# Every third low part of the mixers' streamed weights moves from VectorE to GpSimd

## The chip, the cores and the metric

The kernel runs on one core of a Trainium2 chip. The core's engines each run their own queue of instructions in order: TensorE (PE in the profile, its weight loads PEld) multiplies matrices, VectorE (DVE), ScalarE (ACT) and GpSimd (POOL) do elementwise work, SyncE (SP) issues transfers. They wait for each other through semaphores. The metric is the device time of one execution in microseconds (us), before and after the change.

## What is computed

The reference runs four layers of a transformer in fp32 on 256 tokens of width 1024 (and 256 context tokens in the first two layers). Two layers come from a diffusion-like model with modulated norms, each of a half FFN, a mixer and another half FFN; two come from a decoder with squared-ReLU MLPs. Cut to what matters:

```python
x, ctx = half_ffn(x), half_ffn(ctx)
x += gate * mixer_ab(...)              # AB: grouped attention and latent attention
x = half_ffn(half_ffn(x))
x += gate * mixer_cd(...)              # CD: gated linear recurrence and neighbourhood attention
x = half_ffn(x)                        # the end of the first block
x = x + cat(nsa_attention(rope(rmsnorm(h @ a_w_in))), memory_attention(...)) @ a_w_out   # NSA
x = x + square(relu(rmsnorm(x) @ w_up)) @ w_down
x = x + cat(dilated_attention(rope(...)), memory_attention(...)) @ b_w_out               # DIL
x = x + square(relu(rmsnorm(x) @ w_up)) @ w_down
```

All projections in it are products of activations with weights that are read once from HBM.

## The kernel before

**Products.** A matmul in fp32 is made of three in the type float32r, which TensorE takes faster. Each operand is split into a high part and a low part, its rest: `h` is the value cast to float32r, `l` the value minus `h`. `mm3` (L326) then adds `h.h`, `h.l` and `l.h` into one PSUM tile (L328 to L330 in the profile; with `wh`, `wl` the two parts of weights and `xh`, `xl` those of activations).

**Streamed weights.** `weight` (L310) fetches a unit of up to 1024 columns with one DMA into a tile `raw` (L306, on SP's queue) and cuts it into slices of up to 512 columns. For each slice, `split` (L299) has ScalarE copy the high part `wh` (L300) and VectorE subtract the low part `wl` (L301). There are three buffers `raw`, and nine each of `wh` and `wl` (`RAW, WBUFS = 3, 9`). A buffer `raw` may be loaded again when both parts of its slices have been made; a buffer `wl` may be filled again when the matmuls that read it are done. The whole kernel makes 1064 low parts of weights.

**Stages.** The program runs ada and the first FFNs, then mixer AB (375 to 640 us of the span), two FFNs, mixer CD (1365 to 1740), an FFN, mixer NSA (1905 to 2090), an MLP, mixer DIL (2285 to 2470), and a last MLP. FFNs and MLPs are long rows of matmuls. The mixers have short chains between the engines as well: norms of heads (`ssq`, `ssk` by VectorE's `sumsq_heads`, `rsy`, `rsa` for the reciprocal root), `bmul` (L770) for the scaling of heads, `gmul` and `rope` (L775, L790: products with the sine at L797, with the cosine at L778, the sum at L805 or, written twice over, at L808), transposes at L814, softmax and attention.

**NSA around 1965 us.** Its keys are projected from the weights `n_g1`; `rest` (L1789) takes the heads' norm `rk` from VectorE (`norm_of`, L1664) and has GpSimd scale both halves `kx` and rotate them into the free residual tile `xr1` (twelve instructions on GpSimd: two at L773, ten in four ropes). TensorE meanwhile multiplies with the next weights `n_g2` (units of 768 columns, cut to slices of 384), and does two smaller jobs: the compression's products (`at<-raw,PT`, L1851, whose weights `n_w1` also go through a `raw` buffer, but are not split) and the attention to memory (`at<-mk,qa`, L882; `po<-PT,mv`, L906). Then come the weights `n_g3`, in slices of 512.

**DIL around 2315 us.** Query heads and keys come in two halves of tokens each. `heads` (L2147) gives the first half's scaling and rope to GpSimd and the second half's to VectorE (`eng[t]`).

**Who sets the order.** The code calls the instructions in one order; a scheduler then reorders them per engine, by its own estimate of what is ready when, and only a few places are pinned by `keep_in_program_order`. So where a low part stands in its engine's queue isn't written in the code. On the chip every engine runs its list strictly in order.

Of the kernel before, what the change touches and what calls it, by code (L numbers as in the profile page):

```python
# [3 lines left out]

# [1 line left out]

# [4 lines left out]
F32 = mybir.dt.float32  # L11
# [4 lines left out]
ALU = mybir.AluOpType  # L16
# [220 lines left out]
class Later:  # L237
    def __init__(self, make):
        self.make, self.made = make, None
# [7 lines left out]
class Kern:  # L247
    def __init__(self, tc, es, a):
        self.tc, self.nc, self.es, self.a = tc, tc.nc, es, a
        self.const = self.pool("const", 1)  # L250
        self.res = self.pool("res", 1)
        self.wp = self.pool("wp", WBUFS)
        self.st = self.pool("st", 4)
        self.sq = self.pool("sq", 2)
        self.ps = self.pool("ps", 3, space=PSUM)
        self.ident = self.const.tile([P, P], F32, name="ident")
        self.gv = self.const.tile([P, 13, KC], F32, name="gv")
        self.cols = self.const.tile([P, 3], F32, name="cols")
        self.ones = self.cols[:, 0:1].to_broadcast([P, P])
        self.flip = False  # L260
        self.filler = iter(())
        self.norms = []
        self.logs = False
        self.xr = [self.res.tile([P, KC, 256], F32, name=f"xr{h}") for h in range(2)]
        self.xh = self.res.tile([P, KC, 512], F32R, name="xh")
        self.xl = self.res.tile([P, KC, 512], F32R, name="xl")
# [29 lines left out]

    def split(self, h, l, src):  # L299
        self.nc.scalar.copy(h, src)  # L300
        self.nc.vector.tensor_tensor(l, src, h.bitcast(F32), op=ALU.subtract)  # L301

    def raw(self, ap=None, n=1024):
        r = self.wp.tile([P, 1024], F32, name="raw", tag="raw", bufs=RAW)[:, :n]
# [4 lines left out]
    def weight(self, ap, cut=512):  # L309

        n = ap.shape[-1]
        r = self.raw(ap, n)
        parts = []
        for c0 in range(0, n, cut):
            m = min(cut, n - c0)
            h, l = (self.wp.tile([P, 512], F32R, name=x, tag=x)[:, :m] for x in ("wh", "wl"))
            self.split(h, l, r[:, c0 : c0 + m])
            parts.append((h, l))

        def at(c):  # L320
            j = c.start // cut
            return [v[:, c.start - j * cut : c.stop - j * cut] for v in parts[j]]

        return at
# [1949 lines left out]
def program(tc, a):  # L2274
    with ExitStack() as es:
        k = Kern(tc, es, a)
        with ExitStack() as ada:
            k.ada_start(ada)
            k.begin()
            k.ffn(0, 0, 2, (0, 1), (0, 2, 3, 2), (0, 3, 9, 2))  # L2280
            k.mixer_ab()
            k.ffn(0, 1, 2, (1, 0), (1, 0, 5, 2))
            k.ffn(1, 0, 2, (1, 1), (1, 5, 9, 1))
        k.mixer_cd()
        k.mem_open()
        k.filler = k.mem_steps(0)
        k.ffn(1, 1, 1, None)
        k.mixer_nsa()
        k.filler = k.mem_steps(1)
        k.mlp(0)  # L2290
        k.mixer_dil()
        k.mlp(1)
        for d in range(KC):
            tc.nc.sync.dma_start(a["out"][:, d], k.xr[0][:, d])
# [19 lines left out]
```

## Time and profile before

| | |
|---|---|
| median of 3 runs | 2627.84 us (2619.73 to 2628.19) |
| the profiled execution | 2626.76 us |
| its span in the profile | 2625.0 us |
| mean granted clock of TensorE | 0.982 |
| TensorE, VectorE, ScalarE, GpSimd busy | 2508.2, 1797.3, 1258.7, 405.7 us |

The span runs from the first instruction to the last. An engine's busy time counts only its own work, so the rest of the span is waiting. The trace also has each instruction's start, length and, in brackets, the idle time before it with what ended that. Rows that carry several instructions of one kind (x2, x8) give the time from the start of the first to the end of the last.

### The profile page before, as it was taken

The numbers are of one execution on the slowest core, as the hardware profiler recorded it, in microseconds if no ns is written. First come the engines' busy times: TensorE is split into PE (matmuls) and PEld (weight loads), VectorE is DVE, ScalarE is ACT, GpSimd is POOL, SyncE is SP. The second block draws the span as 40 slices with busy tenths as digits, with TensorE's granted clock in tenths as the row PEclk, the third lists the DMA queues.
The fourth block names the chain that finished last, engine by engine and source line by source line (L and its number), as shares of the span: only waits on it lengthen the run. The fifth ranks groups of instructions, "written<-read, shape, count | busy, mean of one in ns | idle before, by whom it ended". The sixth has DMA issues, their size and how long they took to land. (4 is left out here: it accounts for less than half of the span.)

```text
span 2625.0 us, 40838 instructions
## 1 busy us (share of the span) xinstructions
PE 2508.2 (96%) x14931; PEld 2163.8 (82%) x14931; DVE 1797.3 (68%) x3664; ACT 1258.7 (48%) x2646; POOL 405.7 (15%) x457
## 2 busy tenths in 40 slices
PE   6999999999999999999999998989998899988999
PEld 4888888777888888788888887789986789977999
DVE  4999536787997336843336568866677776788765
ACT  3332235665423234233236667555555665665653
POOL 3000004201100003000003234120023211132111
PEclk7999999999999999999999999999998999999999
DMA  7777332120675334843333221346652255542554
GB/s 267 229 236 233 121 95 67 55 66 28 219 241 169 96 97 134 284 126 98 97 97 93 89 85 33 98 142 197 185 181 86 70 189 185 180 146 71 180 185 145
DMA packets 114474, 367.23 MB, mean 140 GB/s; under 512 B 13600, under 2 KB 23776, under 8 KB 112864
## 3 DMA queue, kind: packets, MB, share of 16 engines
q1 hardware_dynamic: 114272, 364.61, 43.5%
q8 instruction: 118, 1.93, 0.3%
q14 instruction: 84, 0.69, 0.1%
HBM read 363.51 MB, written 1.05 MB: 139 GB/s over the span
## 5 line engine op out<-in xcount | busy, mean ns | idle before, releaser
L300 ACT CAST wh<-raw 128x512 fp32r<-128x512 f32 (+3 forms) x1064 | 636.8, 608 | 905.4 <-PE ps L329 737.4
L301 DVE TENSOR_TENSOR wl<-raw,wh 128x512 fp32r<-128x512 f32 (+3 forms) x1064 | 741.9, 705 | 425.0 <-ACT wh L300 408.4
L329 PE MATMUL ps<-xl,wh 128*128 128x256 f32 (+1 forms) x2384 | 794.2, 334 | 11.9 <-POOL xl L573 5.1
L328 PE MATMUL ps<-xh,wh 128*128 128x256 f32 (+1 forms) x2384 | 791.1, 334 | 14.4 <-ACT xh L566 4.2
L330 PE MATMUL ps<-xh,wl 128*128 128x256 f32 (+1 forms) x2384 | 790.3, 332 | 0.9 <-DVE wl L301 0.9
L329 PEld LDWEIGHTS ps<-xl,wh 128*128 128x128 f32 x2384 | 456.5, 192 | 60.8 <-POOL xl L573 7.4
L328 PEld LDWEIGHTS ps<-xh,wh 128*128 128x128 f32 x2384 | 454.7, 192 | 61.0 <-ACT wh L300 5.1
L330 PEld LDWEIGHTS ps<-xh,wl 128*128 128x128 f32 x2384 | 456.4, 192 | 43.5 <-DVE wl L301 2.1
L328 PE MATMUL ps<-hh,wh 128*128 128x256 f32 (+1 forms) x1312 | 416.6, 318 | 3.9 <-ACT hh L300 3.9
L329 PE MATMUL ps<-hl,wh 128*128 128x256 f32 (+1 forms) x1312 | 416.6, 318 | 0.2
L330 PE MATMUL ps<-hh,wl 128*128 128x256 f32 (+1 forms) x1312 | 415.8, 317 | 0.0
L520 POOL TENSOR_TENSOR acc<-acc,sq 128x256 f32<-128x256 f32 x119 | 98.2, 827 | 1387.3 <-ACT sq L519 1382.7
L446 DVE CUSTOM_DVE_ANT_0 prod<-aw,crow,adab 128x1024 f32<-128x1024 f32 x224 | 287.3, 1282 | 8.1 <-DMA aw<-ada_t 6.6
L328 PEld LDWEIGHTS ps<-hh,wh 128*128 128x128 f32 x1312 | 247.9, 189 | 21.5 <-ACT hh L300 4.3
L329 PEld LDWEIGHTS ps<-hl,wh 128*128 128x128 f32 x1312 | 247.9, 189 | 18.5 <-DVE hl L301 1.4
L330 PEld LDWEIGHTS ps<-hh,wl 128*128 128x128 f32 x1312 | 247.9, 189 | 16.9
L328 PE MATMUL ps<-wh,xh 128*128 128x512 f32 (+4 forms) x464 | 179.5, 387 | 1.9 <-ACT xh L1583 1.9
L329 PE MATMUL ps<-wl,xh 128*128 128x512 f32 (+4 forms) x464 | 176.8, 381 | 4.2 <-DVE wl L301 4.2
L330 PE MATMUL ps<-wh,xl 128*128 128x512 f32 (+4 forms) x464 | 175.6, 379 | 0.0
L592 DVE SCALAR_TENSOR_TENSOR xr<-ps,hgate,xr 128x256 f32<-128x256 f32 x168 | 75.5, 480 | 74.9 <-PE ps L330 74.4
L300 ACT CAST hh<-s 128x256 fp32r<-128x256 f32 (+1 forms) x158 | 76.9, 487 | 58.7 <-DVE s L642 49.8
L329 PEld LDWEIGHTS ps<-wl,xh 128*128 128x128 f32 x464 | 88.1, 190 | 20.4 <-DVE wl L301 7.1
(490 smaller groups left out, 2747.6 us busy)
## 6 DMA issues: line engine op xcount, KB each, us to landing
raw<-w SPq DMA_DIRECT2D x240, 512.0 KB, 3.7
aw<-ada_t SPq DMA_DIRECT2D x128, 512.0 KB, 4.2
raw<-m_up SPq DMA_DIRECT2D x64, 512.0 KB, 4.1
raw<-m_down SPq DMA_DIRECT2D x64, 512.0 KB, 3.9
raw<-w SPq DMA_DIRECT2D x32, 384.0 KB, 3.8
row<-ada_w SPq DMA_DIRECT2D x8, 1024.0 KB, 13.2
raw<-d_q SPq DMA_DIRECT2D x12, 512.0 KB, 3.7
raw<-ab_g SPq DMA_DIRECT2D x8, 512.0 KB, 3.6
```

Of the source, the lines that this page charges most:

```text
L300: self.nc.scalar.copy(h, src)
L301: self.nc.vector.tensor_tensor(l, src, h.bitcast(F32), op=ALU.subtract)
L328: mm(out, lh, rh, start=start, stop=False)
L329: mm(out, lh, rl, start=False, stop=False)
L330: mm(out, ll, rh, start=False, stop=stop)
L446: v.tensor_tensor_reduce(prod, w, self.crow[:, s], 1.0, self.adab[:, l, j : j + 1], op0=ALU.mult, op1=ALU.add, accum_out=self.mods[l][:, m ...
L520: self.nc.gpsimd.tensor_tensor(acc, acc, t, op=ALU.add)
L592: self.nc.vector.scalar_tensor_tensor(x, pt, gate[:, d : d + 1], x, op0=ALU.mult, op1=ALU.add)
```

## The change

`split` takes an engine for the low part. `weight` counts its slices while a flag says that a mixer's code is being written, and gives the low part of every third of these to GpSimd (`nc.gpsimd`). A context manager sets the flag around the four mixers' calls. High parts stay on ScalarE, all other low parts on VectorE, and nothing else in the code changes. Line numbers of the new file are higher by 1 from L261 on, by 8 or 9 from `raw` on: L301 becomes L302, `mm3`'s lines L337 to L339, L773 becomes L782, L778 L787, L797 L806, L805 L814, L808 L817, L882 L891, L906 L915, L1851 L1860.

```diff
--- before.py
+++ after.py
@@ -1,6 +1,6 @@
 import itertools
 import math
-from contextlib import ExitStack
+from contextlib import ExitStack, contextmanager
 
 import numpy as np
 
@@ -258,6 +258,7 @@
         self.cols = self.const.tile([P, 3], F32, name="cols")
         self.ones = self.cols[:, 0:1].to_broadcast([P, P])
         self.flip = False
+        self.mixing, self.slices = False, itertools.count()
         self.filler = iter(())
         self.norms = []
         self.logs = False
@@ -296,9 +297,16 @@
 
 
 
-    def split(self, h, l, src):
+    def split(self, h, l, src, eng=None):
         self.nc.scalar.copy(h, src)
-        self.nc.vector.tensor_tensor(l, src, h.bitcast(F32), op=ALU.subtract)
+        (eng or self.nc.vector).tensor_tensor(l, src, h.bitcast(F32), op=ALU.subtract)
+
+    @contextmanager
+    def mixer(self):
+
+        self.mixing = True
+        yield
+        self.mixing = False
 
     def raw(self, ap=None, n=1024):
         r = self.wp.tile([P, 1024], F32, name="raw", tag="raw", bufs=RAW)[:, :n]
@@ -314,7 +322,8 @@
         for c0 in range(0, n, cut):
             m = min(cut, n - c0)
             h, l = (self.wp.tile([P, 512], F32R, name=x, tag=x)[:, :m] for x in ("wh", "wl"))
-            self.split(h, l, r[:, c0 : c0 + m])
+            third = self.mixing and next(self.slices) % 3 == 2
+            self.split(h, l, r[:, c0 : c0 + m], self.nc.gpsimd if third else None)
             parts.append((h, l))
 
         def at(c):
@@ -2278,17 +2287,21 @@
             k.ada_start(ada)
             k.begin()
             k.ffn(0, 0, 2, (0, 1), (0, 2, 3, 2), (0, 3, 9, 2))
-            k.mixer_ab()
+            with k.mixer():
+                k.mixer_ab()
             k.ffn(0, 1, 2, (1, 0), (1, 0, 5, 2))
             k.ffn(1, 0, 2, (1, 1), (1, 5, 9, 1))
-        k.mixer_cd()
+        with k.mixer():
+            k.mixer_cd()
         k.mem_open()
         k.filler = k.mem_steps(0)
         k.ffn(1, 1, 1, None)
-        k.mixer_nsa()
+        with k.mixer():
+            k.mixer_nsa()
         k.filler = k.mem_steps(1)
         k.mlp(0)
-        k.mixer_dil()
+        with k.mixer():
+            k.mixer_dil()
         k.mlp(1)
         for d in range(KC):
             tc.nc.sync.dma_start(a["out"][:, d], k.xr[0][:, d])
```

In the order of instructions, 82 low parts leave VectorE's list (1064 before, 982 left) for GpSimd's: 67 of 512 columns, 13 of 384 to 420 and 2 of 256; by mixer 17 in AB, 27 in CD, 18 in NSA, 20 in DIL. The scheduler sets other instructions in a new order as well, mostly by a few places. Three places follow. A name's number tells its tile apart from others of that name.

GpSimd in NSA, before, from the end of the first rope of the keys: the chain `kx`, then the copies `hv` of the compression.

```order
L808 TENSOR_TENSOR xr1_77<-kx_18731,P_18834 128x384
L808 TENSOR_TENSOR xr1_77<-kx_18731,P_18838 128x384
L797 TENSOR_TENSOR P_18843<-kx_18819,ts_18351 128x192
L797 TENSOR_TENSOR P_18847<-kx_18819,tw_18354 128x192
L778 TENSOR_TENSOR kx_18819<-kx_18819,ts_18351 128x192
L778 TENSOR_TENSOR kx_18819<-kx_18819,tw_18354 128x192
L808 TENSOR_TENSOR xr1_77<-kx_18819,P_18843 128x384
L808 TENSOR_TENSOR xr1_77<-kx_18819,P_18847 128x384
L1869 COPY hv_19055<-hT_19053 128x12x16 x2
```

GpSimd there after:

```order
L817 TENSOR_TENSOR xr1_77<-kx_18731,P_18834 128x384
L817 TENSOR_TENSOR xr1_77<-kx_18731,P_18838 128x384
L806 TENSOR_TENSOR P_18843<-kx_18819,ts_18351 128x192
L806 TENSOR_TENSOR P_18847<-kx_18819,tw_18354 128x192
L787 TENSOR_TENSOR kx_18819<-kx_18819,ts_18351 128x192
L787 TENSOR_TENSOR kx_18819<-kx_18819,tw_18354 128x192
L817 TENSOR_TENSOR xr1_77<-kx_18819,P_18843 128x384
L817 TENSOR_TENSOR xr1_77<-kx_18819,P_18847 128x384
L302 TENSOR_TENSOR wl_18884<-raw_18877,wh_18883 128x384
L302 TENSOR_TENSOR wl_19062<-raw_19059,wh_19061 128x512
L302 TENSOR_TENSOR wl_19076<-raw_19069,wh_19075 128x512
L302 TENSOR_TENSOR wl_19092<-raw_19089,wh_19091 128x512
```

The low part `wl_18884` (weights `n_g2`) and three of `n_g3` now stand between the chain and `hv`; two more low parts stand ahead of the chain.

TensorE in NSA, before: the first product with `wl_18884` stands ahead of a group of L1851.

```order
L329 MATMUL ps_18973<-wl_18870,xh_78 128x384
L330 MATMUL ps_18973<-wh_18869,xl_79 128x384
L328 MATMUL ps_18973<-wh_18873,xh_78 128x384
L329 MATMUL ps_18897<-wl_18884,xh_78 128x384
L1851 MATMUL at_18618<-raw_18910,PT_18531 64x256
L1851 MATMUL at_18618<-raw_18910,PT_18533 64x256
L1851 MATMUL at_18618<-raw_18910,PT_18531 64x256
L1851 MATMUL at_18618<-raw_18910,PT_18533 64x256
L330 MATMUL ps_18897<-wh_18883,xl_79 128x384
L328 MATMUL ps_18897<-wh_18889,xh_78 128x384
L329 MATMUL ps_18897<-wl_18890,xh_78 128x384
L330 MATMUL ps_18897<-wh_18889,xl_79 128x384
```

TensorE there after:

```order
L915 MATMUL po_18921<-PT_18803,mv_15582 64x256
L915 MATMUL po_18921<-PT_18764,mv_15583 64x256
L915 MATMUL po_18921<-PT_18803,mv_15583 64x256
L891 MATMUL at_18956<-mk_15904,qa_18946 128x256 x4
L338 MATMUL ps_18973<-wl_18874,xh_78 128x384
L339 MATMUL ps_18973<-wh_18873,xl_79 128x384
L891 MATMUL at_18998<-mk_15963,qa_18947 128x256 x3
L1860 MATMUL at_18618<-raw_18910,PT_18531 64x256
L1860 MATMUL at_18618<-raw_18910,PT_18533 64x256
L1860 MATMUL at_18618<-raw_18910,PT_18531 64x256
L1860 MATMUL at_18618<-raw_18910,PT_18533 64x256
L338 MATMUL ps_18897<-wl_18884,xh_78 128x384
```

The first product with `wl_18884` has moved back, behind three products of `po`, seven of `at<-mk,qa`, a pair with the weights 18873 and 18874 and the group with `raw_18910`.

GpSimd in DIL, before: the rope of the first half's keys `x_23075`, then that of the queries `x_23213`.

```order
L337 TENSOR_TENSOR rsy_23082<-ssv_23079,cols_75 128x2
L773 TENSOR_TENSOR x_23075<-x_23075,rsy_23092 128x512
L797 TENSOR_TENSOR P_23101<-x_23075,tk_22992 128x512
L778 TENSOR_TENSOR x_23075<-x_23075,tk_22992 128x512
L808 TENSOR_TENSOR xr1_77<-x_23075,P_23101 128x1024
L773 TENSOR_TENSOR x_23213<-x_23213,rsy_23217 128x512
```

GpSimd there after:

```order
L346 TENSOR_TENSOR rsy_23082<-ssv_23079,cols_75 128x2
L302 TENSOR_TENSOR wl_23155<-raw_23148,wh_23154 128x512
L302 TENSOR_TENSOR wl_23171<-raw_23168,wh_23170 128x512
L782 TENSOR_TENSOR x_23075<-x_23075,rsy_23092 128x512
L806 TENSOR_TENSOR P_23101<-x_23075,tk_22992 128x512
L787 TENSOR_TENSOR x_23075<-x_23075,tk_22992 128x512
L817 TENSOR_TENSOR xr1_77<-x_23075,P_23101 128x1024
L302 TENSOR_TENSOR wl_23185<-raw_23178,wh_23184 128x512
L302 TENSOR_TENSOR wl_23314<-raw_23311,wh_23313 128x512
L302 TENSOR_TENSOR wl_23328<-raw_23321,wh_23327 128x512
L782 TENSOR_TENSOR x_23213<-x_23213,rsy_23217 128x512
L806 TENSOR_TENSOR P_23226<-x_23213,tq0_22995 128x512
```

Two low parts stand ahead of the keys' rope and three behind it; `wl_23185` follows its last instruction.

On SP the loads keep their places nearly everywhere. That of `raw_18940` (`n_w1`), the third load after `raw_18877` (the source of `wl_18884`), waits for GpSimd besides VectorE now, and the loads of `raw_18986` and of the weights `n_g3` stand behind it.

## Rows read from the trace of the kernel before

**Rows 1.** The page, part 1: each engine's busy time, share, instructions.

```profile
PE 2508.2 (96%) x14931; PEld 2163.8 (82%) x14931; DVE 1797.3 (68%) x3664; ACT 1258.7 (48%) x2646; POOL 405.7 (15%) x457
```

**Rows 2.** Windows, NSA, DIL, sum: length, PE, PEld, DVE, ACT, POOL busy, clock, DMA.

```profile
1905.00:2090.00 185.00, 164.80 (x991) 130.01 (x989) 137.79 (x433) 102.75 (x270) 45.82 (x55) 0.92 0.35 112
2285.00:2470.00 185.00, 167.46 (x1062) 144.17 (x1062) 155.82 (x367) 116.88 (x263) 53.53 (x62) 0.97 0.41 131
sum 1010.00, PE 935.42 PEld 773.18 DVE 748.31 ACT 618.75 POOL 278.62; mean PE 233.85 PEld 193.30 DVE 187.08 ACT 154.69 POOL 69.66
```

**Rows 3.** Waits of TensorE in NSA: total, times, longest.

```profile
PE ps L328 <- DVE ssq L745: 3.8, 1, 3.8
```

**Rows 4.** TensorE's timeline in DIL: start, length, instruction, idle before and releaser.

```profile
2314.23 0.50 PE L329 MATMUL ps<-wl,xh 128*128 128x512 f32 x1 [0.96 <-DVE wl L301]
...
2322.11 0.90 PE L814 MATMUL at<-ident,xr 128*128 128x128 f32 x3 [3.61 <-DVE xr L808]
...
2345.36 0.50 PE L329 MATMUL ps<-wl,xh 128*128 128x512 f32 x1 [0.87 <-DVE wl L301]
```

**Rows 5.** VectorE's groups by line and shape: busy us, mean ns of one.

```profile
L301 DVE TENSOR_TENSOR wl<-raw,wh 128x512 fp32r<-128x512 f32 x984 | 702.5, 720 | 417.1 <-ACT wh L300 401.0 <-PE ps L330 8.3
```

**Rows 6.** GpSimd's timeline in DIL, ropes of two `x`.

```profile
2315.39 2.73 POOL L808 TENSOR_TENSOR xr<-x,P 128x1024 f32<-128x1024 f32 x1
...
2344.83 1.61 POOL L805 TENSOR_TENSOR x<-x,P 128x512 f32<-128x512 f32 x1
```

**Rows 7.** VectorE's timeline in DIL, two pairs of low parts.

```profile
2312.41 3.46 DVE L301 TENSOR_TENSOR wl<-raw,wh 128x512 fp32r<-128x512 f32 x2
...
2325.28 1.29 DVE L301 TENSOR_TENSOR wl<-raw,wh 128x512 fp32r<-128x512 f32 x2
```

**Rows 8.** GpSimd's groups by line and shape, 512 and 384 columns.

```profile
L773 POOL TENSOR_TENSOR x<-x,rsy 128x512 f32<-128x512 f32 x4 | 5.3, 1324 | 29.5 <-DVE rsy L345 22.1 <-ACT wh L300 7.4
...
L808 POOL TENSOR_TENSOR xr<-kx,P 128x384 f32<-128x384 f32 x4 | 4.5, 1134 | 0.0
```

**Rows 9.** GpSimd's timeline in NSA, start and end of the `kx` chain.

```profile
1964.99 2.54 POOL L773 TENSOR_TENSOR kx<-kx,rk 128x384 f32<-128x384 f32 x2 [21.49 <-DVE rk L1667]
...
1973.92 2.50 POOL L808 TENSOR_TENSOR xr<-kx,P 128x384 f32<-128x384 f32 x2
```

**Rows 10.** VectorE's timeline in NSA, around `rk`.

```profile
1964.22 0.54 DVE L301 TENSOR_TENSOR wl<-raw,wh 128x384 fp32r<-128x384 f32 x1
1964.68 0.17 DVE L1667 COPY rk<-rsy 128x12 f32<-128x12 f32 x1
```

**Rows 11.** TensorE's timeline in NSA, around the first use of `wl_18884`.

```profile
1964.90 0.33 PE L328 MATMUL ps<-wh,xh 128*128 128x384 f32 x1
1965.07 0.34 PE L329 MATMUL ps<-wl,xh 128*128 128x384 f32 x1
1965.34 1.08 PE L1851 MATMUL at<-raw,PT 128*64 128x256 f32 x8
...
1967.43 1.08 PE L906 MATMUL po<-PT,mv 128*64 128x256 f32 x6
...
1968.89 0.62 PE L882 MATMUL at<-mk,qa 128*128 128x256 f32 x4
...
1970.92 0.51 PE L882 MATMUL at<-mk,qa 128*128 128x256 f32 x3
1972.15 1.08 PE L1851 MATMUL at<-raw,PT 128*64 128x256 f32 x8 [0.72 <-DMA raw<-n_w]
...
1976.93 0.39 PE L329 MATMUL ps<-wl,xh 128*128 128x512 f32 x1
```

**Rows 12.** DMA issues: count, KB each, median us from issue to landing.

```profile
raw<-n_w SPq DMA_DIRECT2D x8, 512.0 KB, 4.0
```

**Rows 13.** Windows of 10 us in DIL, same columns.

```profile
2310.00:2320.00 10.00, 7.07 (x30) 5.06 (x28) 9.42 (x13) 6.14 (x12) 6.87 (x4) 1.00 0.50 158
2320.00:2330.00 10.00, 7.89 (x36) 6.68 (x37) 8.50 (x18) 5.20 (x12) 4.35 (x3) 0.83 0.48 152
```

## The prediction

> **What bounds the kernel now.** I read the table of engines first, then the windows of the four mixers, then the waits and the timelines of single engines there. TensorE is busy for 96% of the span, VectorE for 68%, GpSimd for 15% [rows 1]. So a change of low parts can win only what TensorE idles, and lose whatever it makes TensorE wait. The windows narrow this to the mixers: over their 1010 us TensorE is busy for 935.42 us and idles for 1010 - 935.42 = 74.6 us, while VectorE is busy for 748.31 us (74%) and GpSimd for 278.62 us (28%) [rows 2]. In NSA's window 185 - 164.80 = 20.2 us are idle, in DIL's 185 - 167.46 = 17.5 us. The longest single waits are for small VectorE work at the end of a chain, such as 3.8 us for a sum of squares [rows 3], and 3.61 us for `xr` in DIL [rows 4]. TensorE runs its matmuls in a fixed order, so one late low part holds everything behind it.
>
> **What the change removes from VectorE.** The order of the changed kernel has 82 low parts on GpSimd, 67 of them of 512 columns. One takes VectorE 0.72 us [rows 5], so at most 82 x 0.72 = 59 us leave it, 59/748 = 7.9% of its work in the mixers. If all of TensorE's idle time there were VectorE's and shrank in that share, 0.079 x 74.6 = 5.9 us would come back. That is the far end of this term. The near end is none, because GpSimd's work seems to slow VectorE's: in DIL two low parts took 3.46 us while GpSimd worked on `x`, and two took 1.29 us when it was free for most of them [rows 6, 7]. GpSimd gets 82 more instructions. Nothing of their form and width (two operands from SBUF, a subtraction into float32r, 512 columns) stands on GpSimd before; the nearest by width are a 512-column product at 1.32 us and a 384-column sum at 1.13 us [rows 8], so 82 x 1.32 = 108 us at most, on an engine that idles for 731 us of these windows. Between 0 and -5.9 I take **-3.0**, the middle, since both effects have rows.
>
> **What it moves: a slice behind a long chain.** GpSimd runs in order, so a low part placed there waits for what stands ahead of it. For most of the 82 that is short. In NSA it isn't. The low part `wl_18884` (384 columns) stands directly behind the twelve instructions that build the keys `kx`. Those start at 1964.99, released by VectorE's `rk` after 21.49 us of idling, and end at 1973.92 + 2.50 = 1976.42 [rows 9]. The slice's low part is made on VectorE at 1964.22, just ahead of `rk` at 1964.68 [rows 10], so `rk` may come 0.54 us earlier at best; in the new order another low part stands near it instead, so I leave the start alone. With the subtraction at 1.13 us [rows 8] the low part is ready at 1977.5. If the chain began 0.54 us earlier and the subtraction took the 0.54 us that VectorE needs [rows 10], it would be 1976.4.
>
> TensorE takes this low part at 1965.07 [rows 11]. The new order sets some matmuls ahead of it, which fill part of the wait: three of the first `po` group (half of the 1.08 us of six), four `at` of `mk` (0.62 us), a pair from `wl_18874` (0.45 us, by the 0.17 us from 1964.90 to 1965.07 and the 0.27 us from there to 1965.34, where the form changes), three more `at` (0.51 us) and the `L1851` group, 1.08 us [rows 11]. That is 0.54 + 0.62 + 0.45 + 0.51 + 1.08 = 3.2 us. The 0.72 us that TensorE waits for a transfer at 1972.15 [rows 11] disappears inside the new wait. All of NSA up to the first matmul of the next weights (1976.93) [rows 11] therefore comes later by 1977.2 (between the two ends, nearer the later) - 1965.07 - 3.2 - 0.72 = 8.2; I carry **+8.0**, with ends 1976.4 - 1965.07 - 3.92 = 7.4 and 1977.5 - 1965.07 - 3.92 = 8.5. The end of the mixer hangs on that order of matmuls, so I pass the whole delay on. The 3.8 us wait for a sum of squares [rows 3] follows matmuls of this same row, so it moves with them.
>
> **The transfers behind it.** There are three buffers `raw`. Buffer reuse now makes the load of `raw_18940` wait for GpSimd, since its buffer is that of `wl_18884`, and on SP the next loads are queued behind it. From issue to landing such a load takes 4.0 us [rows 12]. Issued at 1977.3 it lands at 1981.3. TensorE has some eighteen short matmuls ahead of the group that needs it, about 3.2 us at 0.17 to 0.18 each (the step from 1964.90 to 1965.07 [rows 11]), so 1980.4: +0.9 there, and the reuse of that buffer for the next weights may cost as much again. I take **+1.5**, between 0 (the loads are ahead) and 3.
>
> **TensorE's clock.** In DIL, TensorE waits 3.61 us before 2322.11 [rows 4], and the slice from 2320 to 2330 has a granted clock of 0.83, that before it 1.00 [rows 13]. A mean of 0.83 between the levels 2.4 and 1.2 GHz is (1 - 0.83)/0.5 = 34% of 10 us, 3.4 us at 1.2 GHz. Matmuls issued in them take twice as long, so 3.4 us of clock cost up to 1.7 us. A new wait of 8 us should do at least that: **+1.7**, from 0 to 3.4 (twice).
>
> **The same in DIL, CD and AB.** In DIL `wl_23185` stands behind a rope that ends at 2315.39 + 2.73 = 2318.12 [rows 6]; with 1.2 us it is ready at 2319.3, where TensorE takes it at 2314.23 [rows 4]. But TensorE waits until 2322.11 for `xr` later anyway [rows 4]; what it does before that wait starts at 2322.11 - 3.61 = 2318.5 takes 4.3 us at most, so from 2319.3 it ends by 2323.6: 0 to +1.5, I take +0.6, as some of the 4.3 is waiting too. `wl_23477` follows a rope that ends at 2344.83 + 1.61 = 2346.44 [rows 6], ready at 2347.6 against 2345.36 [rows 4]: up to 2.2, partly hidden, +1.0. Together **+1.6**, 0 to 3.7. At the start of AB and of CD one low part, 1.3 us by the 512-column row [rows 8], now stands ahead of the norm's last sums, whose result the next matmuls wait for. Whether its weights are there early decides between 0 and 1.3 each; I take **+0.7** for the two, 0 to 2.6.
>
> **Sum.** 8.0 + 1.5 + 1.7 + 1.6 + 0.7 - 3.0 = +10.5 us. The profiled execution took 2626.76 us, 1.1 us under the median of 2627.84 shown, so I add to it: 2626.76 + 10.5 = 2637.3, forecast **2637 us**. With all terms at their good ends it is 7.4 - 5.9 = +1.5, 2628; at their bad ends 8.5 + 3 + 3.4 + 3.7 + 2.6 = +21.2, 2648.
>
> **Rivals.** *The delay is paid back.* While TensorE waits for `wl_18884`, VectorE and ScalarE run ahead on low parts and softmax; when TensorE resumes, the 20.2 us that it idles in NSA [rows 2] shrink. If half of the 8.0 us is met so, with neither clock nor transfer cost, it is 4.0 + 1.6 + 0.7 - 3.0 = +3.3: 2630. Against it: the later waits follow TensorE's own products; for it: VectorE's load is high there. This counts as no change.
>
> *Faster: VectorE is the bound in dense stretches.* From 2310 to 2320 VectorE is busy for 9.42 of 10 us while TensorE idles 2.9 [rows 13]. If in NSA and DIL, where 38 of the 82 slices lie, TensorE's idle time goes with VectorE's queue, the 38 x 0.72 = 27 us taken off can shorten the 37.7 us of idling there by up to half that, 13.7 us, while the `kx` chain starts early enough to leave 4 us of the delay: 2626.8 - 13.7 + 4.0 = 2617. This decides if waits for VectorE fall by more than the delay adds. Against it: the two engines slow each other [rows 6, 7].
>
> *Slower still: both engines block each other.* The pair of low parts at 2312.41 took 3.46 - 1.29 = 2.17 us more than the one at 2325.28 [rows 7], 1.09 each, while GpSimd was in its rope [rows 6]. If each of the 82 new GpSimd instructions costs VectorE that much, 89 us come on while 59 go: the term -3.0 turns round, to (89 - 59)/748 x 74.6 = +3.0, and where the chain's small steps are hit as well some 4 us more come on: 2626.8 + 13.5 + 3 + 4 = 2647. The Trainium skill, "SBUF — State Buffer", section "Who interferes with whom", states the rule: a VectorE instruction with two SBUF inputs contends with a GpSimd instruction that reads SBUF, and the pair of ports is an exclusive lock, not shared bandwidth. A low part has two such inputs; the 3.46 us pair agrees with the rule, and it speaks against the change.
>
> That the change doesn't do what it says is excluded by the 82 rows of the order.
>
> **How the numbers follow.** Forecast 0.42, paid back 0.36, faster 0.12, blocking 0.10. A measurement can tell about 0.3%, 7.9 us, from no change, so slower means above 2635.7 and faster below 2619.9. The forecast and blocking give slower 0.52, the payback same 0.36, the dense case faster 0.12. The range from 2622 to 2649 leaves out most of the faster case and the far edge of the blocking one; the forecast's own range is 2628 to 2648.
>
> **What would show it.** In the changed profile TensorE should stand before one low part around 1969 for about 8 us, released by GpSimd, with the granted clock down behind it; the `kx` chain should start near 1965 as now; NSA's window should be some 10 us longer, the other mixers within 2 us. VectorE's low parts should keep near 0.72 us: well over 0.8 speaks for blocking. The prediction is wrong if no wait over 3 us released by GpSimd appears in NSA, or if it is there and later waits shrink by as much.

## The result, and the profile after

The changed kernel takes 2660.2 us (2653.59 to 2663.4), the kernel before 2626.2 us beside it: a ratio of 1.0125, interval 1.0111 to 1.014: 33 us slower by the ratio, 34 by the two medians. The forecast was slower by 10, with 2649 as the end of its range. The profiled execution of after has a span of 2651.8 us, 26.8 more than before; it is the shortest of the four executions of after, so the trace shows 27 of the 33 us.

The page's first part, to set against [rows 1]:

```profile
PE 2514.3 (95%) x14931; PEld 2165.2 (82%) x14931; DVE 1789.9 (67%) x3582; ACT 1260.1 (48%) x2646; POOL 510.3 (19%) x539
```

VectorE has 82 instructions fewer, worth 59 us at 0.72 us each (and 55.1 in the run relief below), and its busy time fell by only 1797.3 - 1789.9 = 7.4 us. GpSimd's grew by 104.6. So some 48 to 52 us of VectorE's time were given back, as instructions that take longer.

Where the time went is found by setting the start of the same matmul in the two traces side by side. The difference is -0.2 us ahead of AB and 5.8 behind it; 5.5 ahead of CD, 13.4 behind; 19.8 behind NSA; 20.6 ahead of DIL, 26.8 behind. Nearly all of these 26.8 us are lost in the four mixers, 6 to 8 us in each, and the FFNs and the MLP between them are as long as before within 1 us. The windows of the mixers in after, cut at those matmuls (columns as in [rows 2]: length, then busy time of PE, PEld, DVE, ACT, POOL, then the clock):

```profile
374.80:645.80 271.00, 257.93 (x1473) 207.16 (x1472) 189.02 (x462) 153.37 (x374) 75.79 (x92) 0.99 0.18 55
1370.50:1753.40 382.90, 348.96 (x2127) 293.18 (x2126) 260.13 (x520) 246.05 (x541) 159.24 (x150) 0.97 0.26 83
1918.40:2109.80 191.40, 164.76 (x990) 129.75 (x989) 135.60 (x415) 103.12 (x270) 68.21 (x73) 0.93 0.34 108
2305.60:2496.80 191.20, 168.75 (x1061) 144.15 (x1060) 155.62 (x346) 117.42 (x263) 79.89 (x82) 0.96 0.40 126
```

In DIL, VectorE is as busy as before, 155.62 us against 155.82 [rows 2], with 21 instructions fewer.

**The forecast wait is there.** GpSimd's and then TensorE's timeline in NSA (start, length, instruction, idle time before and what ended it):

```profile
1979.07 2.00 POOL L782 TENSOR_TENSOR kx<-kx,rk 128x384 f32<-128x384 f32 x2 [5.39 <-DVE rk L1676]
...
1987.98 1.94 POOL L817 TENSOR_TENSOR xr<-kx,P 128x384 f32<-128x384 f32 x2
1989.88 0.99 POOL L302 TENSOR_TENSOR wl<-raw,wh 128x384 fp32r<-128x384 f32 x1
```

```profile
1990.93 0.69 PE L338 MATMUL ps<-wl,xh 128*128 128x384 f32 x1 [6.69 <-POOL wl L302]
1991.41 0.52 PE L339 MATMUL ps<-wh,xl 128*128 128x384 f32 x1
1991.73 0.52 PE L337 MATMUL ps<-wh,xh 128*128 128x384 f32 x1
```

The twelve instructions and the low part follow each other without a gap, as in the order, and TensorE stands for 6.69 us. Behind that its matmuls start every 0.32 us where they took 0.17 [rows 11]; the window from 1990 to 2000 shows a mean granted clock of 0.69, between the levels 2.4 and 1.2 GHz:

```profile
1990.00:2000.00 10.00, 9.07 (x43) 7.51 (x44) 2.71 (x10) 2.37 (x6) 0.87 (x1) 0.69 0.58 199
```

**Blocking is there too.** In DIL, GpSimd's and VectorE's timelines in after:

```profile
2337.05 2.67 POOL L817 TENSOR_TENSOR xr<-x,P 128x1024 f32<-128x1024 f32 x1
2339.68 1.26 POOL L302 TENSOR_TENSOR wl<-raw,wh 128x512 fp32r<-128x512 f32 x1
```

```profile
2337.44 2.30 DVE L352 SCALAR_TENSOR_TENSOR rsa<-rsy 128x8 f32<-128x8 f32 x1
2339.77 1.19 DVE L353 TENSOR_TENSOR rsa<-rsa,ssk 128x8 f32<-128x8 f32 x1
2340.99 0.17 DVE L354 SCALAR_TENSOR_TENSOR rsy<-rsa,rsy 128x8 f32<-128x8 f32 x1
```

Two steps on eight columns take 2.30 and 1.19 us, where the third takes 0.17. The first ends at 2339.74, when GpSimd's rope ends (2339.72), the second at 2340.96, when GpSimd's low part ends (2340.94). They are steps of the chain on which the second half's rope, and then TensorE's transposes, hang. Before, one step of the same chain was held up as well, to the end of the same rope; new is the 1.19 us beside the low part:

```profile
2315.79 2.36 DVE L757 TENSOR_SCALAR ssk<-ssk 128x8 f32<-128x8 f32 x1
```

In this execution TensorE doesn't wait for that chain, since it stands for the low part itself, which follows the rope on GpSimd:

```profile
2340.99 0.80 PE L338 MATMUL ps<-wl,xh 128*128 128x512 f32 x1 [5.49 <-POOL wl L302]
```

In CD it does wait for a held step. GpSimd, VectorE and TensorE there, where TensorE waited 0.64 us before:

```profile
1400.34 1.26 POOL L302 TENSOR_TENSOR wl<-raw,wh 128x512 fp32r<-128x512 f32 x1
1400.42 1.18 DVE L353 TENSOR_TENSOR rsa<-rsa,ssv 128x2 f32<-128x2 f32 x1
1401.86 0.80 PE L551 MATMUL at<-ident,rsy 128*128 128x128 f32 x4 [2.47 <-DVE rsy L354]
```

Over the whole trace of after, each VectorE instruction can be set against the median length of its operation with its shapes. Of the TENSOR_TENSOR instructions that begin while a GpSimd instruction runs, 110 of 195 take at least 0.15 us longer than that, of all others none of 1534. TENSOR_SCALAR: 37 of 62 against 3 of 190. Reductions that read PSUM: 0 of 30. The added time of all such instructions is 116 us, against 82 before. GpSimd's own 457 other instructions take 406 us together, against 410 before: in sum they aren't slowed.

### The profile page after: what moved, and what is told of

It reads as the page before. It is cut to its first block, busy times and chain, and to the rows that moved or that the text cites. A ratio compares the mean times of both kernels' runs of the same rounds, so it can differ in the third digit from the quotient of the medians.

```text
span 2651.8 us, 40898 instructions
## 1 busy us (share of the span) xinstructions
PE 2514.3 (95%) x14931; PEld 2165.2 (82%) x14931; DVE 1789.9 (67%) x3582; ACT 1260.1 (48%) x2646; POOL 510.3 (19%) x539
## 5 line engine op out<-in xcount | busy, mean ns | idle before, releaser
L301 ACT CAST wh<-raw 128x512 fp32r<-128x512 f32 (+3 forms) x1064 | 636.8, 608 | 915.4 <-PE ps L338 751.4
L302 DVE TENSOR_TENSOR wl<-raw,wh 128x512 fp32r<-128x512 f32 (+2 forms) x982 | 703.2, 722 | 433.1 <-ACT wh L301 419.8
L337 PE MATMUL ps<-xh,wh 128*128 128x256 f32 (+1 forms) x2384 | 791.0, 334 | 10.9 <-ACT xh L575 4.1
L339 PE MATMUL ps<-xh,wl 128*128 128x256 f32 (+1 forms) x2384 | 789.8, 332 | 1.5 <-DVE wl L302 0.9
L337 PEld LDWEIGHTS ps<-xh,wh 128*128 128x128 f32 x2384 | 454.0, 191 | 58.6 <-ACT wh L301 4.9
L339 PEld LDWEIGHTS ps<-xh,wl 128*128 128x128 f32 x2384 | 456.0, 191 | 44.7 <-DVE wl L302 1.9
L337 PE MATMUL ps<-hh,wh 128*128 128x256 f32 (+1 forms) x1312 | 417.5, 318 | 3.4 <-ACT hh L301 3.4
L339 PE MATMUL ps<-hh,wl 128*128 128x256 f32 (+1 forms) x1312 | 416.7, 318 | 0.0
L337 PEld LDWEIGHTS ps<-hh,wh 128*128 128x128 f32 x1312 | 248.8, 190 | 20.9 <-ACT hh L301 3.8
L339 PEld LDWEIGHTS ps<-hh,wl 128*128 128x128 f32 x1312 | 248.6, 189 | 17.1
L337 PE MATMUL ps<-wh,xh 128*128 128x512 f32 (+4 forms) x464 | 180.2, 389 | 1.9 <-ACT xh L1592 1.5
L339 PE MATMUL ps<-wh,xl 128*128 128x512 f32 (+4 forms) x464 | 177.5, 383 | 0.0
L302 POOL TENSOR_TENSOR wl<-raw,wh 128x512 fp32r<-128x512 f32 (+4 forms) x82 | 110.6, 1350 | 202.9 <-ACT wh L301 173.6
```

The source lines that it names most:

```text
L302: (eng or self.nc.vector).tensor_tensor(l, src, h.bitcast(F32), op=ALU.subtract)
L337: mm(out, lh, rh, start=start, stop=False)
L339: mm(out, ll, rh, start=False, stop=stop)
```

## The experiments

Two theories. **Lateness**: low parts stand behind GpSimd's chains and TensorE waits for them. **Blocking**: GpSimd's instructions hold up VectorE's, whoever waits for their result. The runs, with the kernel before beside them in each set (2627.2, 2626.5 and 2627.6 us), and the busy time of the profiled execution:

| run | us | ratio (interval) | VectorE busy | GpSimd busy |
|---|---|---|---|---|
| before | 2626.2 to 2627.6 | 1 | 1797.3 | 405.7 |
| after | 2660.2 | 1.0125 (1.0111 to 1.014) | 1789.9 | 510.3 |
| late3 | 2645.5 | 1.0070 (1.0055 to 1.0085) | 1788.4 | 504.9 |
| relief | 2602.2 | 0.9907 (0.9891 to 0.9924) | 1742.2 | 397.5 |
| sub | 2671.0 | 1.0164 (1.0149 to 1.0179) | 1845.8 | 519.2 |
| fill | 2636.5 | 1.0035 (1.0021 to 1.0049) | 1802.6 | 508.8 |
| one | 2634.5 | 1.0031 (1.0016 to 1.0046) | 1811.8 | 464.3 |
| twice | 2641.5 | 1.0066 (1.0040 to 1.0091) | 1843.7 | 411.7 |
| nsa17 | 2626.0 | 0.9991 (0.9981 to 1.0002) | 1794.6 | 425.4 |
| ffn10 | 2637.2 | 1.0039 (1.0025 to 1.0053) | 1774.5 | 514.0 |
| ropes | 2611.4 | 0.9948 (0.9926 to 0.9970) | 1811.2 | 306.6 |
| acts | 2627.5 | 1.0003 (0.9990 to 1.0015) | 1772.9 | 405.6 |
| ropes_third | 2644.7 | 1.0074 (1.0052 to 1.0096) | 1808.7 | 414.0 |
| ropes_acc | 2606.1 | 0.9926 (0.9901 to 0.9950) | 1823.6 | 208.8 |

Each edit also lets the scheduler set a new order, and one trace's stages can differ by 2 to 4 us without a cause in the edit: CD is 2.6 us longer in nsa17, and the FFNs between AB and CD are 4.3 us shorter in twice, though these edits change no instruction there.

**late3: the three latest low parts stay on VectorE.**

```diff
-            third = self.mixing and next(self.slices) % 3 == 2
+            at_slice = next(self.slices) if self.mixing else 0
+            third = at_slice % 3 == 2 and at_slice not in (161, 203, 218)
```

> As the changed kernel, but three low parts stay on VectorE: the one behind the kx chain in NSA (wl_18884) and the two that stand right behind a rope in DIL (wl_23185, wl_23477). In the changed kernel TensorE waits 6.7, 5.5 and 2.8 us for them, 15.0 us. Lateness theory (the loss comes from low parts queued behind chains): about 12 us under the changed kernel, so some 2648 where the changed one has 2660, and NSA and DIL end close to the kernel before. Blocking theory (GpSimd and VectorE hold each other up everywhere): the three waits go, but the waits for VectorE return in part, 5 to 8 us under the changed kernel, some 2653; AB and CD keep their 6.0 and 7.8 us either way.

It came 14.7 us under after by the medians (6.4 by the traced executions), nearest to the 12 of lateness, and still 18 above before. Lateness is real: NSA, by the same matmuls, is now 3.7 us shorter than before. But DIL stays 6.1 longer though its two late parts are gone, and AB and CD stay 5.9 and 10.3 longer. What is left in those three has another cause. In DIL the wait for the chain shown above takes the place of that for the late low part: TensorE now stands 4.56 us for `xr`, and 3.61 before [rows 4].

**relief: every third low part isn't made.**

```diff
+            if third:
+                self.nc.scalar.copy(h, r[:, c0 : c0 + m])
+                l = h
+            else:
+                self.split(h, l, r[:, c0 : c0 + m])
```

> As the kernel before, but every third low part of the mixers is not made at all: the matmuls read the high part in its place, so part of the product is left out. It takes 59 us of work off VectorE and gives GpSimd nothing: the pure relief. My term said -3.0 (0 to -5.9): 2623. If VectorE's queue were the bound in dense stretches, -10 to -14: 2614. If relief is worth nothing, 2626 within 2.

-25.0 us, for 55.1 us off VectorE: 0.45 us for each. That is four times the far end of my term, and beyond the -14 of the dense stretches too. TensorE idles 74.6 us in the mixers, and a third of this goes with 7.9% of VectorE's work. (The run also leaves out TensorE's wait from a slice's high part to its low part, so part of the 25 may be that.)

**sub: GpSimd repeats every third subtraction, and nobody reads it.**

```diff
+            s = r[:, c0 : c0 + m]
+            self.split(h, l, s)
+            if third:
+                self.nc.gpsimd.tensor_tensor(s, s, h.bitcast(F32), op=ALU.subtract)
```

> As the kernel before, every low part on VectorE, and GpSimd repeats the subtraction of every third slice in place, in the raw buffer that nobody reads again: 82 instructions of the same form and at the same places as in the changed kernel, but no matmul waits for them. Lateness theory: 2626 to 2632, only raw buffers come free later. Blocking theory: each costs VectorE time and delays GpSimd's own chains, 12 to 25 us slower than before, 2638 to 2651.

+43.8 us, the slowest of all runs and far beyond the 25 of the blocking theory, though every low part that a matmul reads comes from VectorE. No lateness of a GpSimd low part can do that. VectorE's busy time grows by 48.5 us with the same instructions. TensorE's largest waits in sub (total, times, longest), behind those for the `ada` rows at the start, are for VectorE and ScalarE:

```profile
PE ps L341 <- DVE wl L302: 10.4, 13, 2.0
PE ps L340 <- ACT wh L301: 9.9, 8, 2.8
PE at L902 <- DVE P L869: 7.9, 11, 2.0
PE at L554 <- DVE rsy L357: 6.0, 4, 1.9
```

Before, the first of these was 4.2 us in four waits.

**fill: the same places, but GpSimd only writes.**

```diff
-                self.nc.gpsimd.tensor_tensor(s, s, h.bitcast(F32), op=ALU.subtract)
+                for v in (s, s, s[:, : m // 2]):
+                    self.nc.gpsimd.memset(v, 0.0)
```

> As sub, but in place of the subtraction GpSimd fills the same columns of the raw buffer with zeros, two and a half times, about as long as a subtraction (0.5 us for 512 columns by the fill of 1024 in 0.95): the same places in the queue, writing only, no read from SBUF. If GpSimd's longer queue is the cause (its own chains start later), the same as sub, 2638 to 2651. If it is reads of both engines that block each other, VectorE's low parts stay at 0.72 us and the time near 2630, within 5 us.

+9.3 us, 2636.5: a little over the 2635 that I had set for reads as the cause, and under the 2638 for the queue, so against those two numbers the time alone doesn't decide. Set against sub's 43.8, it does. The first part of the page for sub, then for fill:

```profile
PE 2523.7 (95%) x14931; PEld 2173.4 (81%) x14931; DVE 1845.8 (69%) x3664; ACT 1258.4 (47%) x2646; POOL 519.2 (19%) x539
```

```profile
PE 2511.7 (95%) x14931; PEld 2166.9 (82%) x14931; DVE 1802.6 (68%) x3664; ACT 1258.9 (48%) x2646; POOL 508.8 (19%) x703
```

GpSimd is busy nearly as long in both (113 and 103 us more than before). Where it reads two operands, VectorE's 3664 instructions take 48.5 us longer, where it only writes, 5.3. So 34 of the 43.8 us hang on the reading, and 9.3 on GpSimd's longer queue and the later `raw` buffers. (The subtraction also holds the buffer `wh`, which a fill doesn't; the copy of the next run holds it too and costs less than the fill.) The Trainium skill, "SBUF — State Buffer", section "Who interferes with whom", says that a VectorE instruction with two SBUF inputs contends with a GpSimd instruction that reads SBUF and not with one that only writes; the 48.5 and 5.3 us agree.

**one: GpSimd reads a single operand.**

```diff
-                self.nc.gpsimd.tensor_tensor(s, s, h.bitcast(F32), op=ALU.subtract)
+                self.nc.gpsimd.tensor_copy(s, h.bitcast(F32))
```

> As sub, but GpSimd copies the high part into the raw buffer in place of subtracting: one operand read from SBUF where sub reads two and fill none, at the same places. fill cost +9.3 and left VectorE's busy time at +5 us, sub +43.8 and +48 us. If a single read already holds VectorE up, VectorE's busy time grows by about half a us per us of such GpSimd work and the run takes 15 to 35 us more than before; if only the second operand does, it ends with fill, +5 to +12.

By its time, +6.9 us, it ends with fill, as I expected if only the second operand counts. By VectorE's busy time it lies between: that grows by 14.5 us for 58.6 us of GpSimd's, 0.25 for each, where sub has 0.43 and fill 0.05. So a single read seems to block too, about half as much per us, but too little here to show in the time; the copies are also shorter (0.78 us against 1.46 for 512 columns).

**twice: VectorE itself repeats the subtraction.**

```diff
-                self.nc.gpsimd.tensor_tensor(s, s, h.bitcast(F32), op=ALU.subtract)
+                self.nc.vector.tensor_tensor(s, s, h.bitcast(F32), op=ALU.subtract)
```

> As the kernel before, but VectorE itself repeats every third subtraction of the mixers in place, in the raw buffer that nobody reads again: 82 x 0.72 = 59 us more on VectorE, nothing on GpSimd. The opposite of relief, which gave back 25 us for 55. If VectorE's time in the mixers has that price in both directions, +24 to +30, 2652. Then sub's 48 us of lost VectorE time would be worth some 21 of its 44.

13.9 us, where I had 24 to 30; the same subtractions on GpSimd cost 43.8. VectorE's busy time grows by 46.4 us here and 48.5 in sub, so the extra time on VectorE is alike, and its price is 0.30 us per us, under the 0.45 of relief. Of the other 30 us of sub, 9 are GpSimd's queue, by fill. The rest, I think, comes from where VectorE's time falls: held instructions are, among others, the short steps that a transpose or a norm waits for. This I infer from the waits; no run takes the blocking of short steps away alone.

**nsa17: only NSA, without the late part.**

```diff
+            third = at_slice % 3 == 2 and 134 <= at_slice <= 185 and at_slice != 161
```

> The change in NSA alone, without the low part behind the kx chain: 17 low parts on GpSimd, all of NSA's but wl_18884. late3 had the same 17 and its NSA ended 3.7 us sooner than before, while AB, CD and DIL lost 5.9, 10.3 and 6.3. If the stages add up: -3.7, some 2623 where the kernel before has 2627. If the gain in late3's NSA only made up for the delay that came in from CD: 2627 to 2631.

No change (0.9991). The trace has NSA 2.6 us shorter, and CD 2.6 longer, where this run changes nothing. So a gain in NSA isn't shown, only that 17 low parts without a long chain ahead cost nothing there.

**ffn10: as many low parts from the FFNs and MLPs.**

```diff
+            tenth = not self.mixing and next(self.slices) % 10 == 9
+            self.split(h, l, r[:, c0 : c0 + m], self.nc.gpsimd if tenth else None)
```

> The same number of low parts, 81, goes to GpSimd, but from the FFNs, MLPs and the memory projections (every tenth slice there), none from the mixers. If a low part on GpSimd costs in itself (by the reads of both engines), 82 of them cost here what they cost in sub, 20 us or more. If the cost comes from the short chains of the mixers that are held up, 2627 within 3 us: TensorE has a long row of matmuls ahead of each slice here.

Neither number: +10.7 us. By the same matmuls, the long rows lose nothing (8.6 us late at 740 and at 1000 us, 12.55 at 1120 and at 1360). The loss comes in steps near 120, 240, 660, 740, 1030 and 1110 us, where one phase of an FFN hands over to the next and TensorE waits mostly for `hh` and `hl`: 1.17 us at 241.82 and 1.26 us at 243.58, where it doesn't wait before. From 236 to 262 us GpSimd does nothing at all in this run, so these two waits are not its blocking; that the scheduler set the steps of the handover in another order is likely, but wasn't tried apart. So the rows of an FFN lost nothing by low parts on GpSimd; what makes its handovers lose 10 us stays open.

**ropes: the other way round.** In `bmul`, `gmul`, `gmul2`, `rope` and DIL's `eng`, GpSimd is replaced by VectorE; all low parts are on VectorE as before.

```diff
-        (eng or self.nc.gpsimd).tensor_tensor(out, x, r.unsqueeze(2).to_broadcast([P, n, c]), op=ALU.mult)
+        (eng or self.nc.vector).tensor_tensor(out, x, r.unsqueeze(2).to_broadcast([P, n, c]), op=ALU.mult)
...
-        e = eng or self.nc.gpsimd
+        e = eng or self.nc.vector
...
-            eng = (nc.gpsimd, nc.vector)
+            eng = (nc.vector, nc.vector)
```

> The other way round: the kernel before, with the scalings of heads and the ropes of the mixers (bmul, gmul, gmul2, rope) on VectorE in place of GpSimd. Some 115 us leave GpSimd, some 60 us come to VectorE. With the rates of the runs so far (43.8 us more for 113 us of GpSimd work that reads, 25 us less for 55 us off VectorE: 0.39 and 0.45 per us) it is -45 + 27 = -18, 2609. If only VectorE's load counts: +27, 2654.

0.9948, 15 us faster than before, near the -18 of the rates. VectorE takes over 106 instructions. 99 us of GpSimd work went, and VectorE's busy time grew by 13.9 us only; at some 0.6 us each, 106 instructions are about 60. How much of the 15 us is less blocking isn't shown: a rope's own chain is also shorter on VectorE (0.69 us against 1.24 to 1.97 for a product of 512 columns in DIL, before), and no run parts the two.

**acts: relief by ScalarE.**

```diff
-                    self.flip = not self.flip
-                    if self.flip:
-                        nc.scalar.copy(dst, src)
-                    else:
-                        nc.vector.tensor_copy(dst, src)
+                    nc.scalar.copy(dst, src)
```

> The kernel before, with 48 copies of transposed softmax rows (PT, 36 of 512 columns and 12 of 256) on ScalarE where VectorE made them: 30 us leave VectorE for an engine that shares nothing with it in the runs so far. By relief's 0.45 per us: -13, 2614. If ScalarE's queue holds up the exponentials instead: 2627 or more.

No change (1.0003), though VectorE's busy time fell by 24.4 us. So relief's 0.45 isn't a price for any VectorE time: these copies from PSUM inside the softmax chain are worth nothing on ScalarE. That its queue then holds up the next exponentials is my guess from the expectation, and no run shows it.

**ropes_third: ropes and the change together.** Both edits above.

> ropes and the change together: the ropes on VectorE, every third low part of the mixers on GpSimd, which has no chain of ropes ahead of them any more. If lateness behind GpSimd's chains is most of the loss: at ropes' time or under it, 2600 to 2612. If it is the blocking of the two engines: ropes' 2611 + (43.8 - 25), near 2630.

Against lateness, but 15 us over the number for blocking as well. TensorE's waits for GpSimd's low parts fall from 16.4 us (longest 6.7) to 1.9 (longest 0.6), and the change still costs 2644.7 - 2611.4 = 33 us on top of ropes, as much as on top of before. In after, its largest group, and in ropes_third:

```profile
PE ps L338 <- POOL wl L302: 15.8, 6, 6.7
```

```profile
PE ps L338 <- POOL wl L302: 1.3, 4, 0.5
...
PE ps L339 <- POOL wl L302: 0.6, 1, 0.6
```

82 low parts leave VectorE and its busy time falls by 2.5 us, from 1811.2 to 1808.7.

**ropes_acc: the norms' adds on VectorE as well.**

```diff
-            self.nc.gpsimd.tensor_tensor(acc, acc, t, op=ALU.add)
+            self.nc.vector.tensor_tensor(acc, acc, t, op=ALU.add)
```

> ropes, and the adds of the norms' squares (acc, 119 of 256 columns) on VectorE too: 98 us off GpSimd, some 55 us to VectorE. Most of them lie in stretches where TensorE has a long row of matmuls. Where they are the end of a norm's chain VectorE's shorter add gains, so -2 to -8 on ropes' 2611; if VectorE's queue delays them, +3.

0.9926 (0.9901 to 0.9950), 2606.1 us: under both kernels, and by the medians 5 us under ropes, as expected. But the intervals overlap and the two traced spans are alike (2608.8 and 2608.6 us), so the further gain isn't shown. GpSimd's work is halved to 208.8 us, VectorE has 225 instructions more than before and is busy for 26.3 us longer.

## Why the prediction was wrong

**The bound and the sign were right, the size was not.** TensorE idles in the mixers for what ends chains, and slower was the forecast. My terms for lateness, 8.0 + 1.5 + 1.7 + 1.6 + 0.7 = 13.5, are near the 14.7 us that late3 gave back (6.4 by the traced executions, so the nearness is partly luck). What makes the forecast 10 and not 33 is the term for VectorE.

**The late slice in NSA was sized well in its sum.** I had 8.0 + 1.5 + 1.7 = 11.2 us at the first matmul of the next weights. In the traces, the `po` group just ahead of it (1976.02 before, 2000.39 after) is 24.4 us late, of which 13.4 came into NSA: 11.0. The parts fit less well. The low part is ready at 1990.87, which is 1977.5 without those 13.4 us: 8.5 us by my sum. The +1.5 for transfers isn't there, since no wait of TensorE from 1983 to 2022 is for one. The remaining 2.5 would be the clock's, with 0.69 over 10 us, where the row from DIL gave 1.7. The step that failed here is "I pass the whole delay on": NSA ends 6.4 us late, so 4.6 were paid back before its end, as the first rival had it (half of 8.0).

**The term that failed is the relief, -3.0 with ends 0 and -5.9.** It holds two effects that I took as a discount on each other, and each is many times the range. Making fewer low parts on VectorE is worth -25.0 (relief). Running as many subtractions on GpSimd costs +43.8 even if nobody waits for them (sub). Their sum, +18.8, is near what late3 shows, +18.2: the change without its late parts. With the 14.7 us of the three late parts it makes up the whole loss, 33. But the totals agree better than the stages: in AB, CD, NSA and DIL relief and sub add up to 2.0, 14.1, -10.2 and 10.3 us by their traces, and late3 has 5.9, 10.3, -3.7 and 6.1. Nor does the cut hold elsewhere: with the ropes off GpSimd the late waits vanish and the loss stays 33. Why it isn't 18.8 there is open; VectorE gives back 52.6 of relief's 55.1 us there, and 47.7 in after.

Both ends were wrong for a reason. The far end scaled TensorE's idle time with VectorE's share of work (7.9% of 74.6). That prices an us of VectorE at 0.1 us. The runs price it at 0.45 (relief), 0.30 (twice) and nothing (acts), by where it falls. The near end, "none, because GpSimd's work seems to slow VectorE's", stopped at zero with nothing that excluded a loss. The rows for it were in hand: 2.17 us more for a pair of low parts [rows 7]. (The second pair there was not free of GpSimd "for most of them": a product on `x` runs from 2325.50 to 2327.47 beside the pair from 2325.28 to 2326.57. There it is the product that is longer, 1.97 us against 1.24 for the one at 2311.02.) I had priced them in a rival, blocking, at 2647 and a chance of 0.10, by the same scaling by shares: (89 - 59)/748 x 74.6 = 3.0. The 89 us of blocking were too high (48 to 52 us in after, 48.5 in sub), and the price of an us far too low.

**DIL (+1.6) and the norms of AB and CD (+0.7) were too small.** The three mixers lost 6.3, 6.0 and 7.8. In DIL I let the low part's lateness vanish in the 3.61 us wait for `xr`. That wait is gone, but the one for the low part in its place is 5.49 us, and TensorE comes to the transposes of `xr` 3.3 us later than before, where my far end was 1.5. At the second late part it waits 2.78 us, against 0.87 before: 1.9 more, near my far end of 2.2. Without both, in late3, DIL loses as much, in many small waits for VectorE and GpSimd, that for `xr` among them. In AB, the wait for the norm's sums grew from 1.9 to 3.2 us and that for its root from 0.7 to 1.5, within the bound of 1.3 for each place. What I missed is that the same happens at other handovers: the wait for GpSimd's product `aq` grew from 0.9 to 2.5 us. At these three places GpSimd's own step stands directly behind a low part in its queue (the last sum starts at 418.33, as a low part ends at 418.37), so late3 leaves them, and so does a reading by VectorE alone. I had asked which low part comes late, and neither which step of GpSimd comes late behind one nor which short step on VectorE now runs beside one. How the loss of AB and CD divides between these two isn't shown.

**The signs named for blocking did not all show.** For VectorE's low parts, "well over 0.8 speaks for blocking" was a poor test: their mean is 0.73 over the whole kernel, as most lie in FFNs (in the mixers alone it rose from 0.76 to 0.83), while the short steps carry the loss, as I read it. NSA "10 us longer, the other mixers within 2" was wrong for all four: 6.4 and 6 to 8. The signs for the late slice came true: one wait of 6.69 us released by GpSimd, the clock down behind it, and the `kx` chain at its old place, 0.7 us later.

## What to carry to other kernels

Before work moves from VectorE to GpSimd, price the time that GpSimd's reads take from VectorE: here 1.0 us of a GpSimd subtraction took 0.43 us of VectorE's time, so an instruction of 0.72 us that moves and takes 1.41 there frees almost nothing, and some of what is held are short steps on which TensorE waits. Ask as well which of GpSimd's own steps the new work stands ahead of. Bound a term by a run or row at the place, not by shares of busy time, and let no end stop at zero without a reason. Here the gain lay in the opposite direction, from GpSimd to VectorE.

## What the runs showed of the hardware that I had not expected

A step of VectorE on eight columns can take 2.30 us, to the end of the GpSimd instruction beside it, where it else takes 0.15 to 0.17. Reductions on VectorE that read PSUM weren't slowed beside GpSimd (0 of 30), TENSOR_SCALAR instructions, most with their operand in SBUF, were (37 of 62). Fills by GpSimd took almost nothing from VectorE (5.3 us for 103). And 225 instructions more on VectorE raised its busy time by only 26.3 us, while 197 us of GpSimd work beside it went.
